# Native sparse attention on one core: queries produced features-first, mask and maximum in one VectorE operation, a pinned TensorE order

## The chip, the cores and the metric

The kernel runs on one core of a Trainium2 chip. The metric is device time in microseconds (us) of one execution. Engines are named as in the profile: PE is TensorE's matmul, PEld its weight load, DVE is VectorE, ACT is ScalarE, POOL is GpSimd, SP is SyncE (here only an issuer of weight loads). All arithmetic is float32 in result; large projections split each float32 operand into a rounded part and a remainder and add three products (`mm3`: high by high, high by low, low by high), so each weight piece has to be turned into `wh` (by ACT) and `wl` (by DVE) before PE can use it.

## The reference, cut to what matters

Two layers, 256 tokens of 1024 features, 16 heads of 64. Layer 0 is stick-breaking attention and an MLP. Then keys and values of three branches are projected once, and layer 1 uses them in native sparse attention:

```
kv = (rms_norm(h, kv_norm) @ w_kv)                # 3 branches x (k, v) x 4 groups x 64
k_cmp, v_cmp = small MLP over 15 blocks of 32 tokens (cmp_pos, cmp_w1, cmp_w2)
k_slc, k_win = partial_rope(kv[.., 1, 0]), partial_rope(kv[.., 2, 0])
proj = rms_norm(h) @ w_q                          # 1024 query features + 48 gates
q, gates = proj[..., :1024], sigmoid(proj[..., 1024:] + gate_b)
q_rot = partial_rope(q)                           # first 16 of 64 features of each head
p_cmp = softmax(q . k_cmp / 8, blocks that have ended)
p_sel = softmax(q_rot . k_slc / 8, causal)        # 4 blocks of 64: all of them are chosen
p_win = softmax(q_rot . k_win / 8, causal)        # window 512 > 256 tokens
out = (gate0 * p_cmp v_cmp + gate1 * p_sel v_slc + gate2 * p_win v_win) @ w_o
```

After it come layer 1's MLP and a final norm.

## The kernel before

**Weights.** All projection weights go through one list, `stream`, in the order of use. `fetch` (L75) issues a load of 1 MB or less on SP's queue, `split` (L87) makes half a piece's `wh` (L96, ACT) and `wl` (L97, DVE), `W(i)` gives a piece to PE and `step` splits ahead by up to three pieces. Only the first load of the program goes out as two half transfers. The loads of layer 0's value weights are cut by `V_CUT` into four pieces of 512 KB and two of 1 MB.

**Banks.** PSUM tiles of 512 columns come from two pools of four: `bank` and `bank2`. A tile that takes a bank over waits until the one before it there has been read.

**Layer 1's attention, `nsa`** (from 301.89 us to the first MLP matmul at 455.51 us). Its parts, in program order, which the scheduler may rearrange on PE:

- `kv_proj(0..2)`: keys and values of the three branches, 48 products of 512 columns each in three passes; the results for the first 128 tokens go out on ACT and for the second on DVE (`evac`). The transposed hidden state is split into `xk` (for kv) and, from the same PSUM tiles `pt`, into `xq` (for q) by `xt_evac`: high part on ACT, low part on DVE, eight of each.
- `gather_tr`/`gather`, `cw_proj`, `cmp_kv`: the block MLP. `cw_proj` is four pieces of weights for little PE work (16 matmuls of 256 columns each).
- `keys_rope` (POOL) and `keys_tr`: rotated keys, transposed into `kT`, split into two rounded parts.
- `q_proj(0..2)`: queries in three pieces of 304, 384 and 384 columns with tokens on the partitions; the 48 gate columns are in the first. Then per pair of heads `q_unrot` (transposes `ptq` into `qTu`, not rotated, for the block scores) and `q_rope` + `q_rot` (rotation on POOL, a split on ACT and DVE into `qsp`, and transposes `ptr` into `qs`).
- `scores(h)`, per head: six matmuls into `z1` (second 128 tokens, 2 x 256 keys) and `z0` (first 128, 2 x 128 keys), of which two add the causal mask; two DVE maxima (L770, L771); four exps on ACT out of PSUM, each with a sum; `scale(h)` divides by the sum and multiplies by the gate on POOL (L790, two operations).
- `turn(h)`: six transposes `ptp` into two tiles, each copied to SBUF. `values(p)`, per pair of heads: eight matmuls into `po` (each appears as two instructions in the profile) and one for the block branch (`pcT`), then `o_evac` (ACT and DVE).
- `cmp_probs`, `cmp_tr`: block softmax of eight heads for the 15 blocks.
- `out_proj`: 96 matmuls of 512 columns. The last `values` runs inside it.

In the steady part the order is scores(h+1), scale(h), turn(h-1), and values of a pair when its second head has been turned.

**Layer 0.** `proj(p)` makes queries and keys of a pair features-first (queries and keys with features on the partitions, 256 columns), `scores`, `turn`, `values` follow one, two and three pairs behind; the last ones are hooks in `out_proj`, at (half, column half, k).

Of the kernel before, what the change touches and what calls it, by code (L numbers as in the profile page):

```python
# [39 lines left out]
def hybrid_kernel(ctx, tc, x, xcols, eye, gcols, gfin, wqk, wv, wo0, wkv, wqa, wqb, wqc, wo1, w1, w2, cw1, cw2, cpos, gate_b, consts, out):  # L40
# [84 lines left out]
    i_kv = [[feed(wkv[n, i], 2048) for i in range(2)] for n in range(3)]  # L125
    i_c = [[feed(cw1[c, i], 2048) for i in range(2)] for c in range(2)]
    i_q = [[feed(w[i], 4 * n) for i in range(2)] for w, n in ((wqa, 304), (wqb, 384), (wqc, 384))]
    i_o1 = [[feed(wo1[n, i], 2048) for n in range(2)] for i in range(2)]
    i_m.append(feed_mlp(1))

    def mm3(o, a, b, first, last):
        nc.tensor.matmul(o, a[0], b[0], start=first, stop=False, skip_group_check=True)  # L132
        nc.tensor.matmul(o, a[0], b[1], start=False, stop=False, skip_group_check=True)  # L133
        nc.tensor.matmul(o, a[1], b[0], start=False, stop=last, skip_group_check=True)  # L134

    def mm(o, a, b, first, last):
        nc.tensor.matmul(o, a, b, start=first, stop=last, skip_group_check=True)  # L137
# [175 lines left out]
    def layer0(ap):  # L313
# [156 lines left out]
    def nsa(xk, pt0, ap):  # L470
# [18 lines left out]
        rstd = []  # L489

        def kv_proj(n, mid=None):
            pk = [bank(f"pk{t}") for t in range(T)]
            for i in range(2):
                w = W(i_kv[n][i])
                if i and mid is not None:
                    mid()
                for kk in range(4):
                    if n == 0 and i == 0 and kk == 2:
                        pts.append(xt_tr(1))
                        xt_evac(pts[1], 1, 4, xk)  # L500
                    if kk % 2 == 0:
                        step()
                    k = 4 * i + kk
                    for t in range(T):
                        mm3(pk[t], tok(xk, k, t), cut(w, kk * 512, (kk + 1) * 512), k == 0, k == NK - 1)
                if n == 0 and i == 0:
                    rstd.extend([rstd_of(hres[t]) for t in range(T)])
            for t in range(T):
                nk = 512 if n == 0 else 256
                dst = kd0[:, t] if n == 0 else kd[n - 1][t]  # L510
                m = nk // DH
                evac(dst, pk[t][:, 0:nk].rearrange("p (m d) -> p m d", m=m)[:, :, None, :].to_broadcast([P, m, 2, DH]), t)
                if n:
                    evac(vs[t][:, n - 1, :], pk[t][:, 256:512], t)
# [4 lines left out]
        def rope(src, t, n):  # L519

            a = ap.tile([P, n, 16], F32, name="ropea", tag=f"ropea{n}")
            b = ap.tile([P, n, 16], F32, name="ropeb", tag=f"ropeb{n}")
            c = cos[:, t:t + 1, :].to_broadcast([P, n, 16])
            nc.gpsimd.tensor_mul(a, src[:, :, 0:16], c)
            s0 = sin[:, t:t + 1, 0:8].to_broadcast([P, n, 8])
            s1 = sin[:, t:t + 1, 8:16].to_broadcast([P, n, 8])
            nc.gpsimd.tensor_mul(b[:, :, 0:8], src[:, :, 8:16], s0)
            nc.gpsimd.tensor_mul(b[:, :, 8:16], src[:, :, 0:8], s1)
            nc.gpsimd.tensor_add(src[:, :, 0:16], a, b)
# [5 lines left out]
        def gather_tr(c):  # L535
            live["g"] = []
            for gp in range(2):
                pt = bank("ptc")
                for g2 in range(2):
                    g = 2 * gp + g2  # L540
                    for t in range(T):
                        nc.tensor.transpose(pt[:, g2 * 256 + t * P:g2 * 256 + (t + 1) * P],
                                            kd0[:, t, c * NG + g].rearrange("p a d -> p (a d)"), ident)
                live["g"].append(pt)

        def gather(c):
            bt = sp.tile([P, 16, M], F32, name="bt", tag="y")
            b = bt.rearrange("p j (g n) -> p j g n", g=NG)
            for gp, pt in enumerate(live["g"]):
# [11 lines left out]
            nc.vector.tensor_sub(bs[:, :, 1, 0:M], bt, f32(bs[:, :, 0, 0:M]))  # L561
# [3 lines left out]
        def keys_rope(br):  # L565
            for t in range(T):
                rope(kd[br][t].rearrange("p g a d -> p (g a) d"), t, 2 * NG)

        def keys_tr(br):
            for t in range(T):  # L570
                pt = bank("ptk")
                for g in range(NG):
                    nc.tensor.transpose(pt[:, g * P:(g + 1) * P], kd[br][t][:, g].rearrange("p a d -> p (a d)"), ident)
                pv = pt.rearrange("p (g k) -> p g k", g=NG)
                kh = kT[0][:, :, br, t * P:(t + 1) * P]
                nc.scalar.copy(kh, pv)
                nc.vector.tensor_sub(kT[1][:, :, br, t * P:(t + 1) * P], pv, f32(kh))
# [38 lines left out]
        nc.vector.tensor_mul(hu, hx, hx)  # L616
        nc.vector.tensor_scalar(hu, hu, 0.044715, 1.0, op0=OP.mult, op1=OP.add)
        nc.vector.tensor_mul(hu, hu, hx)
# [6 lines left out]

        gates = ap.tile([P, T, 48], F32, name="gates")

        def q_proj(n, mid=None):
            cn = 384 if n else 304
            qn = [ap.tile([P, 384], F32, name=f"q{t}", bufs=2)[:, 0:cn] for t in range(T)]  # L630
            pq = [bank(f"pq{t}") for t in range(T)]
            for i in range(2):
                w = W(i_q[n][i])
                if i and mid is not None:
                    mid()
                for kk in range(4):
                    if kk % 2 == 0:
                        step()
                    k = 4 * i + kk
                    for t in range(T):  # L640
                        mm3(pq[t][:, 0:cn], tok(xq, k, t), cut(w, kk * cn, (kk + 1) * cn), k == 0, k == NK - 1)
            for t in range(T):
                evac(qn[t], pq[t][:, 0:cn], t)
            if n == 0:
                for t in range(T):
                    gt = gates[:, t, :]
                    nc.vector.tensor_add(gt, qn[t][:, 256:304], gbs)
                    nc.vector.tensor_scalar(gt, gt, -80.0, None, op0=OP.max)
                    nc.scalar.activation(gt, gt, AF.Exp, scale=-1.0)
                    nc.vector.tensor_scalar(gt, gt, 1.0, None, op0=OP.add)  # L650
                    nc.vector.reciprocal(gt, gt)
            return qn

        def q_unrot(qn, p0, np_):
            for a in range(0, np_, 2):
                m = min(2, np_ - a)
                pt = bank("ptq").rearrange("p (m q) -> p m q", m=2)
                for j in range(m):
                    for t in range(T):
                        nc.tensor.transpose(pt[:, j, t * P:(t + 1) * P], qn[t][:, (a + j) * P:(a + j + 1) * P], ident)  # L660
                nc.scalar.activation(qT[:, p0 + a:p0 + a + m, :], pt[:, 0:m, :], AF.Copy, scale=0.125)

        def q_rope(qn, nh):
            qsp = []
            for t in range(T):
                qv = qn[t][:, 0:nh * DH].rearrange("p (h d) -> p h d", h=nh)
                rope(qv, t, nh)
                s = ap.tile([P, 6, 2, DH], F32R, name="qsp", bufs=2)[:, 0:nh]
                nc.scalar.activation(s[:, :, 0, :], qv, AF.Copy, scale=0.125)
# [331 lines left out]
```

## Time and profile before

| | |
|---|---|
| time, three runs | 639.6, 641.12, 641.71 us (median 641.12) |
| the profiled execution: own time, span in the profile | 642.27 us, 640.4 us |
| TensorE clock granted, mean | 0.999 of full speed |
| busy: PE, DVE, ACT, POOL | 624.8, 435.6, 350.5, 59.6 us |
| layer 0 attention; its MLP; layer 1 attention; its MLP; end | about 0 to 122; to 301.89; to 455.51; to 627; to 640.4 us |

The time of an execution is some 2 us more than its span (what lies before the first and behind the last instruction). The busy time of a matmul overlaps that of the next one, so what an instruction costs is read from one start to the next.

### The profile page before, as it was taken

Reading aid. Unit: us, or ns where it says so; the run is one execution under the profiler, and the core shown is the slowest. Engines: PE = TensorE matmul, PEld = TensorE weight load, DVE = VectorE, ACT = ScalarE, POOL = GpSimd, SP = SyncE. Lnnn points to the kernel's source line nnn. Section 1 sums busy time; section 2 is a strip of 40 time slices with the busy share of each in tenths; the row PEclk is TensorE's granted clock in tenths of the full one; section 3 lists DMA queues with packets and bytes.
Section 4 is the critical chain, followed back from the end, with each engine's and each line's share of the span. In section 5 each row is a group of like instructions: output and inputs, shape, how many; then the busy total and the mean of one; then the engine's idle time right before and its main releaser. Section 6 shows DMA issues by size and latency. Waiting matters only on the chain.

```text
span 640.4 us, 9068 instructions
## 1 busy us (share of the span) xinstructions
PE 624.8 (98%) x3541; PEld 527.9 (82%) x3541; DVE 435.6 (68%) x632; ACT 350.5 (55%) x606; POOL 59.6 (9%) x100
## 2 busy tenths in 40 slices
PE   9999999999999999999999999999999999999995
PEld 6799986888888888888889987777888888888884
DVE  5587887776566665666899879763776566666554
ACT  5666665464444544444847777752564544454433
POOL 0200000000000000000133344550000000000000
PEclk9999999999999999999999999999999999999999
DMA  8953333446555454553465742001545454555501
GB/s 264 409 211 133 132 132 121 151 174 212 197 182 206 160 208 169 201 190 133 150 253 192 258 156 98 3 2 66 198 168 205 162 204 182 198 198 197 198 0 67
DMA packets 17467, 107.86 MB, mean 168 GB/s; under 512 B 2320, under 2 KB 3088, under 8 KB 5648
## 3 DMA queue, kind: packets, MB, share of 16 engines
q1 hardware_dynamic: 16416, 106.03, 46.6%
q10 hardware_dynamic: 1008, 1.25, 0.5%
q8 instruction: 28, 0.46, 0.3%
q14 instruction: 15, 0.12, 0.1%
HBM read 106.22 MB, written 1.05 MB: 168 GB/s over the span
## 4 chain that ended last, share of the span: by engine, by line
PE 75%; DVE 12%; ACT 4%; DMA 4%; issue 3%; POOL 1%; SPq 0%; POOLq 0%; ACTq 0%; DVEq 0%
PE pu L137 27%; PE acc L132 11%; PE acc L133 11%; PE acc L134 11%; DVE wl L97 5%; PE po L137 2%; DMA raw<-in_wv 2%; DVE sbs L430 2%; PE pk L134 2%; PE pk L132 2%; PE pk L133 2%; ACT wh L96 1%; DVE sbe L424 1%; ACT sbs L429 1%; ACT sbs L428 1%
## 5 line engine op out<-in xcount | busy, mean ns | idle before, releaser
L97 DVE TENSOR_TENSOR wl<-raw,wh 128x1024 fp32r<-128x1024 f32 (+3 forms) x204 | 235.1, 1187 | 125.3 <-ACT wh L96 125.1
L96 ACT CAST wh<-raw 128x1024 fp32r<-128x1024 f32 (+3 forms) x204 | 198.5, 1016 | 118.2 <-PE acc L134 50.9
L137 PE MATMUL pu<-xn,wh 128*128 128x512 f32 x512 | 130.1, 392 | 0.6 <-DVE xn L204 0.6
L137 PEld LDWEIGHTS pu<-xn,wh 128*128 128x128 f32 x512 | 93.8, 188 | 19.6 <-DVE xn L204 1.8
L132 PE MATMUL acc<-wh,hh 128*128 128x512 f32 x256 | 100.2, 391 | 0.0
L133 PE MATMUL acc<-wl,hh 128*128 128x512 f32 x256 | 100.1, 391 | 0.0
L134 PE MATMUL acc<-wh,hl 128*128 128x512 f32 x256 | 99.5, 389 | 0.0
L137 PEld LDWEIGHTS pu<-xn,wl 128*128 128x128 f32 x512 | 71.0, 190 | 5.0
L137 PE MATMUL pu<-xn,wl 128*128 128x256 f32 x512 | 74.0, 282 | 0.0
L134 PEld LDWEIGHTS acc<-wh,hl 128*128 128x128 f32 x256 | 48.1, 188 | 10.6 <-DVE hl L293 0.4
L132 PEld LDWEIGHTS acc<-wh,hh 128*128 128x128 f32 x256 | 48.2, 188 | 9.6 <-ACT hh L292 0.6
L133 PEld LDWEIGHTS acc<-wl,hh 128*128 128x128 f32 x256 | 48.2, 188 | 8.8
L292 ACT CAST hh<-ms 128x512 fp32r<-128x512 f32 x32 | 19.9, 620 | 64.7 <-DVE ms L288 64.7
L286 ACT COPY mr<-pu 128x256 f32<-128x256 f32 x64 | 23.6, 369 | 29.2 <-PE pu L137 29.2
L132 PE MATMUL qk<-xa,wh 128*128 128x256 f32 x128 | 37.0, 289 | 0.0
L133 PE MATMUL qk<-xa,wh 128*128 128x256 f32 x128 | 36.2, 283 | 0.0
L134 PE MATMUL qk<-xa,wl 128*128 128x256 f32 x128 | 36.2, 283 | 0.0
L293 DVE TENSOR_TENSOR hl<-ms,hh 128x512 fp32r<-128x512 f32 x32 | 22.1, 692 | 19.9 <-ACT hh L292 19.9
L287 DVE TENSOR_TENSOR mu<-pu,mr 128x256 f32<-128x256 f32 x64 | 26.7, 418 | 5.8 <-ACT mr L286 5.8
L790 POOL TENSOR_TENSOR pe<-pe,rs 128x256 f32<-128x256 f32 (+1 forms) x32 | 27.1, 866 | 23.6 <-DVE rs L786 19.9
L132 PE MATMUL acc<-wh,oT 128*128 128x512 f32 x64 | 25.8, 403 | 0.0
L132 PEld LDWEIGHTS qk<-xa,wh 128*128 128x128 f32 x128 | 24.5, 191 | 1.0 <-issue 0.9
(187 smaller groups left out, 919.7 us busy)
## 6 DMA issues: line engine op xcount, KB each, us to landing
raw<-in_w SPq DMA_DIRECT2D x64, 1024.0 KB, 4.8
raw<-in_wqk SPq DMA_DIRECT2D x8, 1024.0 KB, 6.5
raw<-in_wo SPq DMA_DIRECT2D x8, 1024.0 KB, 4.8
raw<-in_wkv SPq DMA_DIRECT2D x6, 1024.0 KB, 4.8
raw<-in_cw SPq DMA_DIRECT2D x4, 1024.0 KB, 4.8
raw<-in_wv SPq DMA_DIRECT2D x2, 1024.0 KB, 8.1
raw<-in_wv SPq DMA_DIRECT2D x3, 512.0 KB, 5.6
raw<-in_wqb SPq DMA_DIRECT2D x2, 768.0 KB, 4.1
```

The costliest lines, as they stand in the source:

```text
L96: nc.scalar.copy(h[:, r], raws[j][:, r])
L97: nc.vector.tensor_sub(lo[:, r], raws[j][:, r], f32(h[:, r]))
L132: nc.tensor.matmul(o, a[0], b[0], start=first, stop=False, skip_group_check=True)
L133: nc.tensor.matmul(o, a[0], b[1], start=False, stop=False, skip_group_check=True)
L134: nc.tensor.matmul(o, a[1], b[0], start=False, stop=last, skip_group_check=True)
L137: nc.tensor.matmul(o, a, b, start=first, stop=last, skip_group_check=True)
L286: nc.scalar.copy(r[:, q], pu[f][:, 256:512])
L287: nc.vector.tensor_add(u[:, q], pu[f][:, 0:256], r[:, q])
L292: nc.scalar.copy(hh, sv)
L293: nc.vector.tensor_sub(hl, sv, f32(hh))
L430: nc.vector.tensor_tensor_scan(s[:, ::-1], s[:, ::-1], go_on[:, ::-1], 0.0, OP.add, OP.mult)
L790: nc.gpsimd.tensor_tensor(s, s, rs[:, t, :][:, :, None].to_broadcast([P, 2, n]), op=OP.mult)
```

## The change

1. **Queries.** The weights are cut into four pieces of 2048 columns, one for each group of four heads, and `q_proj(g, half)` produces queries with features on the partitions. Both sets of transposes, the splits of rotated queries and the rotation of queries on POOL fall away. The rotation is now: a DVE shuffle of partitions within 32, a DVE product with a sine table, a POOL product with a cosine table, and a DVE sum. The tables are multiplied by the norm's factor of each token, which two matmuls (`pr`) spread over the partitions.
2. **Gates.** Their weights are loaded apart (on ACT's queue) and split early; `gate_proj` has 32 small matmuls after `kv_proj(1)`.
3. **Order of the weight stream.** Pieces of kv, the block MLP and q alternate, so that the short `cw_proj` pieces are apart. Both `gather_tr` stand in `kv_proj(1)`. The split of the blocks' remainder and the keys' rotation (both token halves in one operation) are on POOL. All evacuations of kv are on ACT.
4. **Scores.** Per pair of heads: four float32 matmuls on half the array's rows each, without mask matmuls and without a split of keys or queries. One custom DVE operation (L792) adds the mask, writes negated masked scores to SBUF and reduces to their minimum, with a second instruction that writes out that result: eight such couples for each pair of heads. The exp reads SBUF.
5. **Turns and values.** `turn(p)` has 12 transposes and three copies of 512 columns; values stand four pairs behind scores, and the last four values and two turns stand in `out_proj`. The block branch's value matmul is cut in two of 64 columns.
6. **Order.** From behind `kv_proj(0)` to the end of the scores loop PE's instructions are kept in program order.
7. **Layer 0.** `turn(NP-2)` moves behind 24 matmuls of `out_proj`, and the first seven weight loads go out as halves.

```diff
-            if len(raws) == 1:
+            if len(raws) <= len(V_CUT) + 1:
                 nc.sync.dma_start(raws[-1][:, 0:n // 2], src[:, 0:n // 2])
                 nc.sync.dma_start(raws[-1][:, n // 2:], src[:, n // 2:])
...
+    def pe(ins):
+        if strict[0]:
+            tc.keep_in_program_order(ins)
...
-        out_proj(oT, i_o0, {(0, 0, 2): [lambda: scores(NP - 1), lambda: turn(NP - 2), lambda: values(NP - 3)],
-                            (0, 1, 1): [lambda: values(NP - 2)],
+        out_proj(oT, i_o0, {(0, 0, 2): [lambda: scores(NP - 1), lambda: values(NP - 3)],
+                            (0, 1, 0): [lambda: turn(NP - 2)], (0, 1, 2): [lambda: values(NP - 2)],
...
-                evac(dst, pk[t][:, 0:nk].rearrange("p (m d) -> p m d", m=m)[:, :, None, :].to_broadcast([P, m, 2, DH]), t)
+                nc.scalar.activation(dst, pk[n][t][:, 0:nk].rearrange("p (m d) -> p m d", m=m)[:, :, None, :]
+                                     .to_broadcast([P, m, 2, DH]), AF.Copy, scale=rstd[t])
...
-            nc.vector.tensor_sub(bs[:, :, 1, 0:M], bt, f32(bs[:, :, 0, 0:M]))
+            nc.gpsimd.tensor_sub(bs[:, :, 1, 0:M], bt, f32(bs[:, :, 0, 0:M]))
...
+        pr = bank2("pr")
+        for t in range(T):
+            mm(pr[:, t * P:(t + 1) * P], rstd[t].to_broadcast([P, P]), ident, t == 0, True)
+        for a in range(2):
+            nc.vector.scalar_tensor_tensor(cs[:, a, :], pr[:, 0:T * P], -1.0, cs[:, a, :], op0=OP.mult, op1=OP.mult)
+        kv_proj(1, 0)
+        gather_tr(0)
+        gather_tr(1)
+        kv_proj(1, 1)
+        gather(0)
+        gather(1)
+        gate_proj()
+        keys_rope(0)
+        ph = bank2("ph")
+        kv_proj(2, 0)
+        cw_proj(0, 0)
+        kv_proj(2, 1)
...
+            if half:
+                pq = live.pop(("q", g)).rearrange("p (j q) -> p j q", j=2)
+                nc.scalar.activation(qu[:, g], pq, AF.Copy, scale=0.125)
+                qx = ap.tile([P, 2, T * P], F32, name="qx", bufs=2)
+                nc.vector.stream_shuffle(qx, qu[:, g], swap)
+                nc.gpsimd.tensor_tensor(qr[:, g], qu[:, g], cs[:, 0:1, :].to_broadcast([P, 2, T * P]), op=OP.mult)
+                nc.vector.tensor_tensor(qx, qx, cs[:, 1:2, :].to_broadcast([P, 2, T * P]), op=OP.mult)
+                nc.vector.tensor_add(qr[:, g], qr[:, g], qx)
...
+        def scores(p):
+            g, j = divmod(p, 2)
+            z1 = [bank2(f"z1{hd}").rearrange("p (b k) -> p b k", b=2) for hd in range(2)]
+            z0 = [bank2(f"z0{hd}")[:, 0:256].rearrange("p (b k) -> p b k", b=2) for hd in range(2)]
+            for t, z in ((1, z1), (0, z0)):
+                for hd in range(2):
+                    r = slice(hd * DH, (hd + 1) * DH)
+                    mm(z[hd], qr[r, g, j, t * P:(t + 1) * P], kT[r, g, :, 0:(t + 1) * P], True, True)
...
+                        nc.vector.tensor_tensor_reduce(e, z[hd][:, b, :], nmask[:, 2 * P - n:2 * P], 1.0, 3e38, OP.add, OP.min,
+                                                       nm[:, hd, t, b:b + 1])
+                        nc.scalar.activation(e, e, AF.Exp, scale=-1.0, bias=nm[:, hd, t, b:b + 1],
+                                             accum_out=rs[:, hd, t, b:b + 1])
...
+        scores(0)
+        q_proj(2, 0)
+        scores(1)
+        got = cmp_kv()
+        q_proj(2, 1)
+        scores(2)
+        cmp_kv2(*got)
+        turn(0)
+        q_proj(3, 0)
+        cmp_probs(0)
+        scores(3)
+        turn(1)
+        q_proj(3, 1)
+        cmp_tr(0)
...
+        for p in range(4, NP):
+            scores(p)
+            values(p - 4)
+            turn(p - 2)
...
+        strict[0] = False
```

What moves on the engines is seen at three places. The first is ACT at the end of `kv_proj(0)`, before: `kd` is the block branch's keys and values out of PSUM (one of two, the other being on DVE), `xq` the high part of the queries' input.

```order
L96 CAST wh<-raw 128x1024
L203 ACTIVATE xq<-pt_2617,gc 128x256
L203 ACTIVATE xq<-pt_2618,gc 128x256
L203 ACTIVATE xq<-pt_2688,gc 128x256
L482 ACTIVATE kd_2658<-pk_2662,r 128x1024
L203 ACTIVATE xq<-pt_2689,gc 128x256
L96 CAST wh<-raw 128x1024 x5
```

The same place of the changed kernel:

```order
L96 CAST wh<-raw 128x1024
L532 ACTIVATE kd_2671<-pk_2676,r 128x1024
L532 ACTIVATE kd_2671<-pk_2677,r 128x1024
L219 ACTIVATE xq<-pt_2623,gc 128x256
L219 ACTIVATE xq<-pt_2624,gc 128x256
L219 ACTIVATE xq<-pt_2702,gc 128x256
L219 ACTIVATE xq<-pt_2703,gc 128x256
L96 CAST wh<-raw 128x1024 x5
```

Both `kd` operations, which need the end of `kv_proj(0)` on PE, now stand ahead of the last four `xq`. On PE of the changed kernel the two `pr` matmuls stand right behind `kv_proj(0)`, and everything of the rest of `nsa` behind them:

```order
L145 MATMUL pk_2677<-wh,xk 128x512
L146 MATMUL pk_2677<-wl,xk 128x512
L147 MATMUL pk_2677<-wh,xk 128x512
L150 MATMUL pr<-ident,r 128x128 x2
L145 MATMUL pk_2806<-wh,xk 128x512
L146 MATMUL pk_2806<-wl,xk 128x512
L147 MATMUL pk_2806<-wh,xk 128x512
```

In the kernel before no such matmul stands there. In the changed kernel `pr` takes the bank of the tile `pt_2623`, whose last reader is the low part of the fifth `xq` on DVE, which follows that `xq` on ACT (a wait on the operation that stands there in the built program).

The second place is POOL from the queries of group 1 to those of group 2 (`qr` is a query group's product with the cosine table, `pe` a pair's probabilities, `hv` a copy for the block branch), in the changed kernel:

```order
L678 TENSOR_TENSOR qr<-qu,cs 128x512 x2
L803 TENSOR_TENSOR pe<-pe,rs 128x512 x2
L803 TENSOR_TENSOR pe<-pe,rs 128x256 x2
L709 COPY hv<-hidT 128x480
L803 TENSOR_TENSOR pe<-pe,rs 128x512 x2
L803 TENSOR_TENSOR pe<-pe,rs 128x256 x2
L678 TENSOR_TENSOR qr<-qu,cs 128x512
```

The scales of pairs 0 and 1 and the copy `hv` stand between the second and third `qr`. Before, POOL had there the scale of one head and the rotation of the third query piece for both halves of the tokens (`q_3349` and `q_3350`):

```order
L790 TENSOR_TENSOR pe<-pe,rs 128x256
L790 TENSOR_TENSOR pe<-pe,rs 128x512
L524 TENSOR_TENSOR ropea<-q_3349,cst 128x96
L527 TENSOR_TENSOR ropeb<-q_3349,cst 128x6x8
L528 TENSOR_TENSOR ropeb<-q_3349,cst 128x6x8
L529 TENSOR_TENSOR q_3349<-ropea,ropeb 128x6x16
```

There, one head's scale stood ahead of the rotation; now it is four heads' scales and a copy.

The third place is DVE of the changed kernel at pair 2's scores (`z_3453` and `z_3454`: the second 128 tokens of its two heads, two branches each; `qx` the shuffled queries of group 2):

```order
L677 STREAM_SHUFFLE qx<-qu 128x512
L792 ISA pe,nm<-z_3453,nmask 128x256
L792 ISA nm 128x1
L679 TENSOR_TENSOR qx<-qx,cs 128x512
L792 ISA pe,nm<-z_3453,nmask 128x256
L792 ISA nm 128x1
L680 TENSOR_TENSOR qr<-qr,qx 128x512
L792 ISA pe,nm<-z_3454,nmask 128x256
L792 ISA nm 128x1
L792 ISA pe,nm<-z_3454,nmask 128x256
L792 ISA nm 128x1
```

Before, DVE had at its scores one maximum for all of a head's `z1` and one for its `z0`:

```order
L770 TENSOR_REDUCE nm<-z_3564 128x2
L771 TENSOR_REDUCE nm<-z_3565 128x2
L784 RECIPROCAL rs<-rs 128x4
L728 TENSOR_REDUCE cmx<-psc 128x8
L786 TENSOR_TENSOR rs<-rs,gates 128x4
```

The sum `qr`, which waits for POOL's third product, now stands ahead of six of pair 2's eight mask-and-maximum operations. PE's `pvc` (the block branch's values), `turn(0)` and all behind them wait for the fourth of these, since `pvc` takes over the bank of `z_3454`.

## Rows read from the trace of the kernel before

**Rows 1.** Busy time by stretch: us, then PE, PEld, DVE, ACT, POOL, PEclk, DMA share, GB/s

```profile
302.00:345.00 43.00, 42.13 (x228) 36.09 (x227) 39.80 (x50) 30.83 (x47) 13.58 (x22) 1.00 0.52 180
345.00:382.00 37.00, 35.44 (x246) 33.20 (x245) 30.99 (x56) 24.68 (x52) 12.29 (x22) 1.00 0.65 228
382.00:400.00 18.00, 16.54 (x135) 13.21 (x136) 16.68 (x52) 13.20 (x49) 9.21 (x13) 1.00 0.23 87
400.00:432.00 32.00, 31.29 (x233) 23.07 (x230) 22.73 (x66) 21.73 (x93) 17.88 (x23) 1.00 0.01 2
```

**Rows 2.** PE's waits from 300 to 456 us: total, times, longest

```profile
PE z L137 <- ACT pe L775: 1.4, 2, 0.7
PE ptk L573 <- POOL kd L529: 0.9, 1, 0.9
```

**Rows 3.** Timeline of PE: start us, duration us, then the instruction; 384-column products, `ptr`

```profile
363.63 0.33 PE L133 MATMUL pq<-wl,xq 128*128 128x384 f32 x1
363.81 0.34 PE L134 MATMUL pq<-wh,xq 128*128 128x384 f32 x1
363.98 0.80 PE L680 MATMUL ptr<-ident_r,qsp 128*128 128x128 f32 x8
364.62 0.62 PE L137 MATMUL pkc<-hidT,w2d 128*128 128x60 f32 x4
```

**Rows 4.** Timeline of PE, steady part of the scores: values, a turn, a head's scores

```profile
415.26 1.60 PE L137 MATMUL po<-pT,vs 128*64 128x256 f32 x16
416.79 0.70 PE L137 MATMUL po<-pcT,vcb 60*128 60x256 f32 x2
417.42 0.33 PE L799 MATMUL ptp<-ident,pe 128*128 128x128 f32 x1
...
418.05 0.71 PE L137 MATMUL z<-kT,qs 128*128 128x512 f32 x2
...
419.09 0.27 PE L799 MATMUL ptp<-ident,pe 128*128 128x128 f32 x1
```

**Rows 5.** Timeline of PE in layer 0: 256-column products, a pair's scores

```profile
71.75 0.28 PE L133 MATMUL qk<-xa,wh 128*128 128x256 f32 x1
71.87 0.28 PE L134 MATMUL qk<-xa,wl 128*128 128x256 f32 x1
72.08 0.92 PE L137 MATMUL z<-qkT 64*128 64x256 f32 x8
72.94 0.44 PE L442 MATMUL pa<-ident,sbe 128*128 128x128 f32 x2
```

**Rows 6.** PE's waits from 0 to 122 us

```profile
PE pv L132 <- ACT wh L96: 1.5, 1, 1.5
...
PE pa L442 <- ACT sbe L432: 1.1, 2, 0.8
```

**Rows 7.** Timeline of ACT: layer 0's split of a 1 MB value piece

```profile
18.37 2.00 ACT L96 CAST wh<-raw 128x1024 fp32r<-128x1024 f32 x2 [2.70 <-DMA raw<-in_wv]
```

**Rows 8.** Timeline of ACT at the end of `kv_proj(0)`

```profile
313.26 1.12 ACT L482 ACTIVATE kd<-pk,r 128x1024 f32<-128x1024 f32 x1
314.28 0.46 ACT L203 ACTIVATE xq<-pt,gc 128x256 fp32r<-128x256 f32 x1
314.63 1.99 ACT L96 CAST wh<-raw 128x1024 fp32r<-128x1024 f32 x2
```

**Rows 9.** Timeline of POOL: the keys' rotation, beside DVE's `wl`

```profile
327.41 1.26 POOL L524 TENSOR_TENSOR ropea<-kd,cst 128x128 f32<-128x128 f32 x1
...
331.27 0.46 POOL L529 TENSOR_TENSOR kd<-ropea,ropeb 128x128 f32<-128x128 f32 x1
```

**Rows 10.** POOL's groups, 300 to 432 us: busy, mean ns, then idle before and releaser

```profile
L790 POOL TENSOR_TENSOR pe<-pe,rs 128x512 f32<-128x512 f32 x16 | 17.1, 1066 | 0.0
L790 POOL TENSOR_TENSOR pe<-pe,rs 128x256 f32<-128x256 f32 x16 | 10.6, 665 | 23.6 <-DVE rs L786 19.9 <-ACT q L482 3.7
```

**Rows 11.** Timeline of DVE: a head's maxima

```profile
404.71 0.68 DVE L770 TENSOR_REDUCE nm<-z 128x2 f32<-128x512 f32 x1
405.31 0.41 DVE L771 TENSOR_REDUCE nm<-z 128x2 f32<-128x256 f32 x1
405.64 0.17 DVE L784 RECIPROCAL rs<-rs 128x4 f32<-128x4 f32 x1
```

**Rows 12.** Groups of DVE (380 to 432 us) and of ACT (302 to 432 us), one each

```profile
L728 DVE TENSOR_REDUCE cmx<-psc 128x8 f32<-128x120 f32 x4 | 1.1, 276 | 0.9 <-PE psc L137 0.8
...
L775 ACT ACTIVATION_READ_ACCUMULATOR pe<-z,nm 128x1 f32 x32 | 6.4, 201 | 0.0
```

**Rows 13.** DVE's group of weight splits, 302 to 382 us

```profile
L97 DVE TENSOR_TENSOR wl<-raw,wh 128x1024 fp32r<-128x1024 f32 x23 | 28.7, 1274 | 2.9 <-ACT wh L96 2.8
```

More of the change, by code (lines that the diff above doesn't have):

```diff
@@ L489, in nsa, with kv_proj @@
         rstd = []
[L491 to L507, printed above, removed]
+        pk = {}
+        def kv_proj(n, i):
+            if i == 0:
+                pk[n] = [bank(f"pk{t}") for t in range(T)]
+            w = W(i_kv[n][i])
+            for kk in range(4):
+                if n == 0 and i == 0 and kk == 2:
+                    pts.append(xt_tr(1))
+                    xt_evac(pts[1], 1, 4, xk)
+                if kk % 2 == 0:
+                    step()
+                k = 4 * i + kk
+                for t in range(T):
+                    mm3(pk[n][t], tok(xk, k, t), cut(w, kk * 512, (kk + 1) * 512), k == 0, k == NK - 1)
+            if n == 0 and i == 0:
+                rstd.extend([rstd_of(hres[t]) for t in range(T)])
+            if i == 0:
+                return
             for t in range(T):
@@ L623, in nsa @@
         nc.vector.tensor_mul(hu, hu, hx)
[L626 to L669, printed above, removed]
-                nc.vector.scalar_tensor_tensor(s[:, :, 1, :], qv, 0.125, f32(s[:, :, 0, :]),
-                                               op0=OP.mult, op1=OP.subtract)
-                qsp.append(s)
-            return qsp
@@ L702, in cmp_kv2 @@
         def cmp_kv2(hidT, hv):
-            pc = bank("pkc")
+            pc = bank2("pkc")
             for e in range(2):
@@ new lines, in cmp_probs @@
+            n = 8 * T
+            pv = pc[:, 0:T * 120].rearrange("p (h n) -> p h n", h=n)
+            mx = ap.tile([P, n], F32, name="cmx")
+            nc.vector.tensor_reduce(mx, pv, axis=AX.X, op=OP.max)
+            e = ap.tile([P, n, NC], F32, name="ce", bufs=2)
+            nc.vector.tensor_tensor(e, pv, mx[:, :, None].to_broadcast([P, n, NC]), op=OP.subtract)
+            for t in range(T):
+                nc.scalar.activation(e[:, 8 * t:8 * t + 8, :], e[:, 8 * t:8 * t + 8, :], AF.Exp, scale=rstd[t])
@@ new lines, in turn @@
+        def turn(p, bk=bank):
+            pes = live.pop(("e", p))
+            pT = ap.tile([P, 12 * P], F32, name="pT", bufs=2)
+            for i in range(3):
+                pt = bk("ptp")
+                for m in range(4):
+                    hb, c = divmod(4 * i + m, 3)
+                    hd, b = divmod(hb, 2)
+                    o = (512 + b * P, b * 256, b * 256 + P)[c]
+                    tr(pt[:, m * P:(m + 1) * P], pes[hd][:, o:o + P])
+                if i == 1:
+                    nc.vector.tensor_copy(pT[:, 512 * i:512 * (i + 1)], pt)
+                else:
+                    nc.scalar.copy(pT[:, 512 * i:512 * (i + 1)], pt)
+            live["t", p] = pT
@@ L809, in values @@
+        def values(p, bk=bank):
             g = p // 2
-            po = bank("po1")
-            pT = [live.pop(("t", 2 * p + hd)) for hd in range(2)]
+            po = bk("po1")
+            pT = live.pop(("t", p))
             for b in range(2):
```

331 lines of the change are left out of this document (149 added, 182 removed).

## The prediction

> **What bounds the kernel now.** I read the busy time by stretch first. PE is the bound nearly everywhere: in layer 1's attention its idle time is 0.87, 1.56, 1.46 and 0.71 us in four stretches up to 432 us, 4.6 us in all, at the full clock (PEclk 1.00, the 2.4 GHz level) [rows 1]. So the change earns what it takes out of PE, and loses what new waits put in. Second, PE's waits: the longest are scores for the exps that free their banks and keys for POOL's rotation [rows 2]. DVE is next in line: 16.68 of 18 us from 382 to 400, but 22.73 of 32 us in the steady part [rows 1]. ACT and POOL have room. Outside this layer two places count: layer 0's start, where PE waits 1.5 us for a split behind a 1 MB load, and one turn that waits 0.8 us [rows 6, 7].
>
> **What goes from PE.** Costs are from start to start.
> - 32 `ptr` transposes: eight take 0.64 us, so 2.6 us [rows 3]. 16 `ptq`: by the turn's six in 0.63 us, 0.105 each, 1.7 us [rows 4].
> - Scores: a head costs 1.04 us now (418.05 to 419.09), a pair 2.08 [rows 4]. The new form is layer 0's: half the rows, no mask; 768 columns take 0.86 us there, so 1536 take 1.72 [rows 5]. The values' 16 instructions, also 1536 columns at half the array, take 1.53 [rows 4]. I take 1.65, nearer the same form: 0.43 a pair, 3.4 us (2.9 to 4.4).
> - The block branch's value matmul: 0.63 us now; as two halves by the values' rate (512 of 1536 columns) 0.51: 1.0 us for eight pairs (0 to 1.0) [rows 4].
> - Query products: 384 columns take 0.17 us, 304 in proportion 0.14, so 96 and 48 of them 23.3 us; 192 of 256 columns at just under 0.12, say 0.118, take 22.7: 0.6 us [rows 3, 5].
> - Added: 32 gate matmuls of 96 or 48 columns. The nearest rows are `ptr` with 0.08 (128 columns) and 0.12 for 256: I take 0.08, 2.6 us (1.3 by columns alone, 3.8) [rows 3, 5]. `pr`, four instructions by a transpose's 0.105: 0.4 us.
>
> Together 6.3 us less work. If nothing new waits, the 4.6 us of idle time go too. Adding the spacings up from 347.55 to 404.35 us leaves some 2.3 us that are neither work nor listed wait, where transposes, scores and block softmax alternate; half of it, 1.2, I count as going (0 to 2.3).
>
> **Layer 0.** With half loads ACT can split the first half of the 1 MB piece before the second lands; of the 1.5 us I take 1.3 (0 if the loads together are limited by the transfer rate) [rows 6, 7]. The moved turn hides its 0.8 us behind 24 products; with it 0.7. Together 2.0 us.
>
> No new wait: 6.3 + 4.6 + 1.2 + 2.0 = 14.1 us less.
>
> **What the new order adds.** PE's order is pinned now, so a wait at its head stops all of it.
> 1. *`pr`.* It follows `kv_proj(0)` and takes a bank whose last reader is the fifth low part of `xq`, which follows ACT's fifth high part. That one now stands behind both `kd` operations, 1.02 us each from start to start, and these need the end of `kv_proj(0)`; the first started at 313.26 [rows 8]. So: 313.3 + 2 x 1.02 + 0.35 for the high part + 0.4 for DVE's part = 316.1, with the releases 316.3, while PE is free at 313.7: 2.6 us (1.6 if `kd` overlaps more, 3.4 if a weight split gets between). Before, one `kd` was on DVE and nothing on PE waited.
> 2. *The first `cw_proj`.* The blocks' remainder stands on POOL behind the keys' rotation (four operations, now twice as long). A rotation step takes 0.46 us alone and 1.26 beside DVE's `wl` [rows 9]. From the end of the key evacuations, some 2 us behind `kv_proj(1)` (four operations of half or a quarter of `kd`'s columns), rotation takes about 5 us and 960 columns of remainder 2.0 (512 take 1.07, rows 10); PE gets there after gates and half of `kv_proj(2)`, 2.6 + 5.5 us. 1.0 us late (0 to 2.5).
> 3. *Pairs 0 to 2.* From the end of the second query chunk as 0: scores of pair 0 to 1.65, half a query chunk (24 x 0.118) to 4.5. Meanwhile DVE has two halves of a weight split (1.27 each [rows 13]), the GELU steps, group 1's rotation and eight mask-and-maximum couples, one after another: I take 0.42 us for 256 columns with its read and 0.30 for 128 (below). The eighth ends at 6.8, another `wl` at 7.9, and the second operation on pair 1's first tile ends at 8.9; `pht` takes over that tile's bank. PE would have been there at 6.1: 2.8 us. Half a chunk and pair 2's scores end at 13.7; `pkc` waits until 15.0 for pair 2's first tile: 1.3 us. Then DVE reaches the sum `qr` of group 2, whose product stands on POOL behind pair 0's scales (from 8.9: 2 x 1.07 + 2 x 0.67 = 3.5), `hv` (0.6), pair 1's (3.5), and its own 1.07 [rows 10]: 17.6. DVE waits for it, from about 14.9, with pair 2's third and fourth operation queued behind; these end at 18.8, and `pvc`, `turn(0)` and the next query chunk stand until then, from 15.5: 3.3 us. Together 7.4 us (5 to 10).
>
> Later pairs: PE per pair 1.65 + 1.53 + 0.51 + 1.26 (12 transposes) = 4.95 us, DVE eight couples for 2.9, a copy of 0.6 and some 0.65 of small ones, 4.15; POOL 3.5; ACT's exps now read SBUF, and it has room. So PE bounds again, and pair 3's and group 3's waits lie behind query products.
>
> **The unknown price** is the mask-and-maximum couple. Lower bound: a maximum of 256 columns starts 0.33 us before the next operation (405.31 to 405.64) and lasts 0.41; 120 columns last 0.28 [rows 11, 12]; with no cost for the read 4 x 0.33 + 4 x 0.22 = 2.2 us a pair. Upper bound: full durations and a read such as ACT's, 0.20 [rows 12]: 4 x 0.41 + 4 x 0.28 + 8 x 0.20 = 4.4. I take 2.9, nearer to DVE's own rows, as DVE shows no read here.
>
> The Trainium skill ("VectorE: DVE Perf Modes", rules for kernel authors and the section on the DRAIN) speaks against this step: fusing is not done for speed, since the pipe empties after each operation, and the number of operations should be kept low. Here the number goes from four maxima a pair to eight couples. Row 405.31 has the next operation 0.08 us before the first one's end, so the trace agrees only in part; by the rule alone the pair would cost the upper bound.
>
> **The sum.** 642.27 (own time of the profiled execution, 1.15 above the median) - 14.1 + 2.6 + 1.0 + 7.4 = 639.2; against the median 638.0. About 0.3% (1.9 us) is what a measurement of this kernel can tell from no change, so this is a small gain, 0.5%.
>
> **The rivals.**
> - *No new wait bites.* If POOL and DVE queue less than I walked, and `pr`'s and `qr`'s waits are short, 14.1 us are won: 627.0 us. For it: DVE has 9.3 us to spare from 400 to 432, POOL 14 [rows 1]. Against: the three waits stand in the built order, and their durations are this trace's. 0.16.
> - *DVE becomes the bound in the scores: slower.* With 4.4 us for the couples DVE needs 5.65 a pair against PE's 4.95: 0.7 for each of the last six pairs, 4.0 us; and the 20 couples ahead of `pvc` cost 1.5/8 more each, 3.7 us. 645.7. It decides from about 3.7 us a pair on; above 3.9 the time is behind the old one. For it: the couple's second instruction, and the pages' rule above. Against: the short rows of DVE. 0.18.
> - *The gain is eaten.* Layer 0 gives nothing since its start is bound by the transfer rate (+2.0), and the gates cost 0.12 each (+1.2): 641.2, no change. 0.16.
>
> **How the numbers follow.** My own case has 0.50, from 634 to 641: 0.40 of it faster by over 0.3% (below 639.2), 0.10 within. With the first rival 0.56 faster; the third (0.14) and my rest 0.24 the same; the second and a little of the third 0.20 slower. The range reaches from the first rival's 626, if all idle time goes, to the second's 645.5: 626 to 645.5.
>
> **What would show it.** Right: PE idle about 2.6 us ahead of `pr` with DVE `xq` as releaser; about 3 us each ahead of `pht` and `pvc`, with DVE's `nm` as releaser, and POOL's product `qr` late; a DVE idle of 2 to 3 us ahead of `qr`; pairs of 5.0 us from pair 4 on, without idle. `pv`'s wait in layer 0 below 0.3 us. Wrong: couples over 0.45 us on average, with PE waiting for `nm` in every pair (the second rival); a scores pair that still takes 2 us; gate matmuls over 0.12; or waits on ACT's exps, to which I gave nothing.

## The result, and the profile after

The changed kernel takes 648.99 us (median of four runs, 647.88 to 650.14) where the kernel before takes 640.54 (639.60 to 641.71): a ratio of 1.0131, 95% interval 1.0105 to 1.0157. It is 8.45 us slower; a gain of 3.1 us was forecast.

The profiled execution (649.01 us, span 647.2, 6.8 above that of before) puts the loss in one place. Layer 1's attention runs from 300.64 to 462.43 us, 161.8 us where it was 153.6; it starts 1.25 us earlier (layer 0), and what follows it takes the same time. First PE's waits in that layer, in the view of [rows 2]:

```profile
PE pvc L150 <- DVE nm L792: 3.8, 1, 3.8
PE pr L150 <- DVE xq L220: 2.9, 1, 2.9
PE pkc L150 <- DVE nm L792: 1.9, 1, 1.9
PE pht L705 <- DVE rs L798: 1.4, 1, 1.4
PE z L150 <- DVE nm L792: 0.7, 2, 0.4
PE z L150 <- ACT pcT L763: 0.2, 1, 0.2
```

10.9 us in all. The four longest stand at places that were walked to, behind the releasers that were named; for `pht` the view names `rs`, which stands on DVE right behind the `nm` that was meant. The fifth place, the first `cw_proj`, has no wait. The second thing was in no term. PE's busy time and granted clock by stretch, with the columns of [rows 1] for PE alone (us, busy, PEclk, DMA share, GB/s):

```profile
300.00:312.00 12.00, 12.00 (x59) 1.00 0.42 141
312.00:316.00 4.00, 1.13 (x5) 0.92 0.74 262
316.00:320.00 4.00, 4.00 (x15) 0.66 0.12 20
320.00:366.00 46.00, 46.00 (x312) 1.00 0.59 221
366.00:382.00 16.00, 12.40 (x80) 1.00 0.39 150
382.00:386.00 4.00, 0.23 (x2) 0.70 0.00 0
386.00:390.00 4.00, 4.00 (x27) 0.50 0.01 4
390.00:394.00 4.00, 4.00 (x35) 0.95 0.00 2
```

Before, PEclk is 1.00 in every stretch of this layer [rows 1]. Now it drops twice towards 0.50 (the 1.2 GHz level): behind the wait ahead of `pr`, and in and behind the waits ahead of `pkc` and `pvc`. PE counts as busy for all of 386 to 390, and does its work at half speed.

The same on PE's timeline (start, duration, the instruction; what it waited in brackets):

```profile
377.92 1.56 PE L150 MATMUL z<-kT,qr 64*128 64x512 f32 x8
381.33 0.63 PE L150 MATMUL pkc<-hidT,w2d 128*128 128x60 f32 x4 [1.85 <-DVE nm L792]
385.77 1.93 PE L150 MATMUL pvc<-cw2s,hv 128*60 128x64 f32 x16 [3.81 <-DVE nm L792]
387.63 2.82 PE L153 MATMUL ptp<-ident,pe 128*128 128x128 f32 x12
```

Twelve transposes take 2.82 us here and 1.53 at full clock later. What DVE and POOL did meanwhile, each on its own timeline, POOL's first:

```profile
374.59 4.16 POOL L803 TENSOR_TENSOR pe<-pe,rs 128x512 f32<-128x512 f32 x4 [5.74 <-DVE rs L798]
378.70 0.59 POOL L709 COPY hv<-hidT 128x480 f32<-128x480 f32 x1
379.25 3.62 POOL L803 TENSOR_TENSOR pe<-pe,rs 128x512 f32<-128x512 f32 x4
382.84 1.26 POOL L678 TENSOR_TENSOR qr<-qu,cs 128x512 f32<-128x512 f32 x1
```

```profile
384.13 0.69 DVE L680 TENSOR_TENSOR qr<-qr,qx 128x512 f32<-128x512 f32 x1 [2.95 <-POOL qr L678]
384.74 0.42 DVE L792 CUSTOM_DVE_ANT_0 pe<-z,nmask 128x256 f32<-128x256 f32 x1
385.08 0.08 DVE L792 DVE_READ_ACCUMULATOR2_ANT nm<- 128x1 f32 x1
385.08 0.42 DVE L792 CUSTOM_DVE_ANT_0 pe<-z,nmask 128x256 f32<-128x256 f32 x1
```

The queries' product of group 2 ran on POOL from 382.84, behind two pairs' scales and `hv`; DVE stood 2.95 us for it, with the two operations for which `pvc` waited queued behind. On ACT the two `kd` stand ahead of the `xq` for which `pr` waited, as in the order shown above:

```profile
312.28 2.15 ACT L532 ACTIVATE kd<-pk,r 128x1024 f32<-128x1024 f32 x2
314.28 1.61 ACT L219 ACTIVATE xq<-pt,gc 128x256 fp32r<-128x256 f32 x4
```

And the work itself, to be read against [rows 4]: the gates and what follows them, the scores of pairs 0 and 1, and a pair in the steady part.

```profile
330.22 3.65 PE L150 MATMUL pg<-wgp,xq 128*128 128x96 f32 x32
333.71 0.49 PE L145 MATMUL pk<-wh,xk 128*128 128x512 f32 x1
...
365.60 1.56 PE L150 MATMUL z<-kT,qr 64*128 64x512 f32 x8
...
370.16 1.12 PE L150 MATMUL z<-kT,qr 64*128 64x512 f32 x2
371.62 1.52 PE L150 MATMUL z<-kT,qr 64*128 64x512 f32 x6 [0.34 <-DVE nm L792]
...
421.79 2.00 PE L150 MATMUL z<-kT,qr 64*128 64x512 f32 x8
423.71 1.52 PE L150 MATMUL po<-pT,vs 128*64 128x256 f32 x16
425.16 0.65 PE L150 MATMUL po<-pcT,vcb 60*64 60x256 f32 x4
425.74 1.53 PE L153 MATMUL ptp<-ident,pe 128*128 128x128 f32 x12
```

### The profile page after: what moved, and what is told of

Its sections match the earlier page's. It is cut to its first block, busy times and chain, and to the rows that moved or that the text cites. A ratio compares the mean times of both kernels' runs of the same rounds, so it can differ in the third digit from the quotient of the medians.

```text
span 647.2 us, 9100 instructions
## 1 busy us (share of the span) xinstructions
PE 625.8 (97%) x3561; PEld 524.7 (81%) x3561; DVE 428.5 (66%) x672; ACT 354.7 (55%) x603; POOL 57.0 (9%) x76
## 4 chain that ended last, share of the span: by engine, by line
PE 81%; ACT 6%; DVE 5%; issue 2%; POOL 2%; DMA 2%; SPq 0%; POOLq 0%; ACTq 0%; DVEq 0%
PE pu L150 27%; PE acc L145 11%; PE acc L146 11%; PE acc L147 11%; PE po L150 3%; DVE wl L97 3%; ACT pe L794 2%; POOL pe L803 2%; ACT wh L96 2%; PE z L150 1%; PE qk L145 1%; PE pk L145 1%; PE pk L146 1%; PE pk L147 1%; PE ptp L153 1%
## 5 line engine op out<-in xcount | busy, mean ns | idle before, releaser
L97 DVE TENSOR_TENSOR wl<-raw,wh 128x1024 fp32r<-128x1024 f32 (+1 forms) x200 | 240.3, 1238 | 120.8 <-ACT wh L96 120.6
L96 ACT CAST wh<-raw 128x1024 fp32r<-128x1024 f32 (+1 forms) x200 | 197.9, 1031 | 104.7 <-PE acc L147 46.4
L803 POOL TENSOR_TENSOR pe<-pe,rs 128x512 f32<-128x512 f32 (+1 forms) x32 | 31.2, 1007 | 27.9 <-ACT pT L820 14.8
L794 ACT ACTIVATE pe<-pe,nm 128x256 f32<-128x256 f32 (+1 forms) x64 | 28.3, 444 | 7.0 <-DVE nm L792 6.9
```

Of the source, the lines that this page charges most:

```text
L96: nc.scalar.copy(h[:, r], raws[j][:, r])
L97: nc.vector.tensor_sub(lo[:, r], raws[j][:, r], f32(h[:, r]))
L794: nc.scalar.activation(e, e, AF.Exp, scale=-1.0, bias=nm[:, hd, t, b:b + 1], accum_out=rs[:, hd, t, b:b + 1])
L803: nc.gpsimd.tensor_tensor(sv, sv, rs[:, hd, t, :][:, :, None].to_broadcast([P, 2, n]), op=OP.mult)
```

## The experiments

Theory: the three waits and the half clock behind them are the loss, and both come from results that are late on ACT, DVE and POOL and meet a PE order that can't step aside. Rivals: the waits are handed on when one is removed; the new work on PE is what costs; the clock falls for another reason.

**e1: `pr` later.**

```diff
-        pr = bank2("pr")
...
         kv_proj(1, 0)
+        pr = bank2("pr")
```

> The two pr matmuls stand behind the first half of kv_proj(1) instead of ahead of it. Waits and clock (my theory): PE's 2.9 us wait ahead of pr goes, and with it the half clock behind it (granted 0.50 from 316 to 318 us, 0.81 from 318 to 320: 1.4 us): 4.3 us less, about 644.7 us. Rival, the wait is only handed on (DVE and ACT are as late for pairs 0 to 2 as before): under 1.5 us less, 647.5 or more, with larger waits ahead of pht, pkc or pvc.

Measured: 643.97 us (642.02 to 646.32), ratio to before 1.0049 (1.0031 to 1.0067): 5.0 us less. No wait ahead of `pr` is left, the waits ahead of `pht`, `pkc` and `pvc` stay at 1.3, 1.8 and 3.8 us. The wait wasn't handed on. (In the trace the clock now fell at another place, from 329 to 333 us; e5 takes that up. Of the ten executions four took 645.6 to 646.3 us with a mean granted clock of 0.989, the traced one among them, and six 642.0 to 644.0 us with 0.991 to 0.994, so such a dip need not stand in every execution.)

**e2: the product on DVE.**

```diff
-                nc.gpsimd.tensor_tensor(qr[:, g], qu[:, g], cs[:, 0:1, :]...
+                nc.vector.tensor_tensor(qr[:, g], qu[:, g], cs[:, 0:1, :]...
```

> The queries' product with the cosine table is on DVE instead of POOL. Waits and clock: DVE no longer waits 2.95 us for POOL ahead of the sum qr, PE's wait ahead of pvc falls from 3.8 to 1.5 us or less, and the half clock from 384 to 390 us (3.4 us lost) goes for the most part: 4 to 6 us less, 643 to 645 us. Rival, DVE is the bound there: the four added operations of 0.6 us keep pvc's wait above 3 us and the time at 648 to 650.

Measured: 650.51 us, ratio 1.0146 (1.0120 to 1.0172); the rival's number, and its wait: `pvc` still waits 4.0 us. PE's listed waits are 10.2 us in all, for 10.9 in the changed kernel; what rose is the loss by the clock, with a mean of 0.981 to 0.984 over the four executions for 0.986 to 0.989. DVE no longer waits for POOL, but it is slowed by it. DVE's timeline of this kernel, beside POOL's scales:

```profile
377.09 3.70 DVE L97 TENSOR_TENSOR wl<-raw,wh 128x1024 fp32r<-128x1024 f32 x2
...
382.75 1.16 DVE L678 TENSOR_TENSOR qr<-qu,cs 128x512 f32<-128x512 f32 x1
383.84 1.52 DVE L679 TENSOR_TENSOR qx<-qx,cs 128x512 f32<-128x512 f32 x1
385.28 0.41 DVE L792 CUSTOM_DVE_ANT_0 pe<-z,nmask 128x256 f32<-128x256 f32 x1
```

Two splits take 3.70 us, and products of 512 columns 1.16 and 1.52, where such a product takes 0.68 and a split 1.21 with POOL idle (changed kernel, 362.46 and 364.38 us). So neither engine's queue had room at that place.

**e3: `pr` later, and the rotation of groups 2 and 3 issued later.** e1's edit is in it; the rotation's four operations now stand in a function, `q_rope`.

```diff
+                if g < 2:
+                    q_rope(g)
...
         turn(0)
+        q_rope(2)
         q_proj(3, 0)
...
             turn(p - 2)
+            if p == 4:
+                q_rope(3)
```

> pr late, and the rotation of the query groups 2 and 3 issued after turn(0) and after turn(2), with its product still on POOL. Waits and clock: both long waits and both stretches of half clock go, 2.9 + 1.4 + 3.8 + 3.4 = 11.5 us less at most, 638 to 640 us, about the kernel before. Rival, the new work on PE is what costs (gates 3.5 us, scores of 1.9 to 2.2 us a pair): the time stays above 644 us.

Measured: 637.68 us (636.49 to 639.88), ratio 0.9954 (0.9937 to 0.9972): 11.3 us less than the changed kernel, and faster than before. PE's largest waits in the layer:

```profile
PE pht L709 <- DVE rs L802: 1.4, 1, 1.4
PE z L150 <- DVE ce L750: 0.8, 1, 0.8
PE pkc L150 <- DVE nm L796: 0.7, 1, 0.7
```

The new work is not what made the kernel slower than before: all of it is still there.

**e4: the idle stretches filled.** Matmuls whose results nobody reads stand in the waits; the waited-for results come no earlier.

```diff
+        fill(12)
         pr = bank2("pr")
...
+            fill(8)
             pc = bank2("pkc")
...
+            fill(16)
             pvc = bank2("pvc")
```

> The changed kernel with idle PE filled: 12 matmuls of 512 columns ahead of pr, 8 ahead of pkc and 16 ahead of pvc, whose results nobody reads. Each fill is about as long as the wait that it stands in, so the waits stay (as work). If the clock falls because of the idle stretches, it now stays at 1.00 and the 4.8 us of half clock come back: about 644 us. Rival, the clock falls for another reason or its loss is hidden: 648 to 650 us, clock still below 1.00 behind the fills.

Measured: 645.59 us (644.29 to 646.20), ratio 1.0064 (1.0039 to 1.0090): 3.4 us less, with more work. The stretches that fell before:

```profile
312.00:316.00 4.00, 3.84 (x19) 1.00 0.57 236
316.00:320.00 4.00, 4.00 (x20) 1.00 0.40 113
...
382.00:386.00 4.00, 3.88 (x37) 1.00 0.00 0
386.00:390.00 4.00, 4.00 (x37) 1.00 0.54 178
```

So the idle time does pull the clock down, and this costs 3.4 us, or rather more: the fills and the waits that are left last about 0.5 us longer together than the waits did. The two timelines agree: from the first `pk` to the first `z` the changed kernel takes 64.96 us and this one 63.41; from there to the first `psc` 27.61 and 25.44: 3.7 us together.

**e5: wide gates on top of e3.** The gates with features on the partitions: 16 matmuls of 256 columns and two transposes for 32 short ones.

```diff
-                    mm(pg[:, t * 96:(t + 1) * 96], h, wgp[:, k].rearrange("p a c -> p (a c)"), k == 0 and t == 0, False)
-                    mm(pg[:, t * 96:t * 96 + 48], lo, wgp[:, k, 0, :], False, k == NK - 1)
+                mm(pg[0:96, 0:256], wgp[:, k].rearrange("p a c -> p (a c)"), xq[0][:, k, :], k == 0, False)
+                mm(pg[0:48, 0:256], wgp[:, k, 0, :], xq[1][:, k, :], False, k == NK - 1)
```

> On top of e3 (637.7 us): the gates are produced features-first, 16 matmuls of 256 columns and two transposes instead of 32 matmuls of 96 or 48 columns. If the short matmuls themselves let the clock fall behind them (0.50 to 0.69 for four microseconds, PE listed as busy all the time), it now stays at 1.00: 1.4 us of work and 1.7 us of clock less, about 634.6 us. Rival, the clock there follows from the earlier short idle or the transposes: only the 1.4 us of work go, 636.3 us, and the dip stays.

Measured: 636.86 us (635.05 to 638.74), ratio 0.9930 (0.9907 to 0.9954); against e3 the intervals overlap, so a gain of 0.8 us is not established. The stretch of the gates, e3's row first and e5's in the fence behind:

```profile
324.00:328.00 4.00, 4.00 (x36) 1.00 0.00 0
328.00:332.00 4.00, 4.00 (x13) 0.57 0.73 262
```

```profile
324.00:328.00 4.00, 4.00 (x27) 1.00 0.05 20
328.00:332.00 4.00, 4.00 (x20) 1.00 0.69 225
```

In e3 PE has no wait there and the clock still fell, right behind 32 matmuls of 96 or 48 columns; in e5 it did not. But e5 lost it at 368 to 372 us (0.57), behind the wait of 1.35 us ahead of `pht`, which in e3 was as long and had left it at 1.00. The expectation was half right: the dip left the gates and came back elsewhere.

**e6: group 1's rotation behind pair 0's scores, on top of e3.**

```diff
-                if g < 2:
+                if g < 1:
                     q_rope(g)
...
         scores(0)
+        q_rope(1)
         q_proj(2, 0)
```

> On top of e3 (637.7 us): the rotation of query group 1 is issued behind the scores of pair 0, so the eight mask-and-maximum operations of pair 0 stand together on DVE. If pair 1's scores and pht wait for DVE's place in its queue, their waits (0.3 + 1.4 us, and 1.2 us inside pair 1's matmuls) fall by about 1.5 us: 636.2 us. Rival, DVE's amount of work in that stretch decides, not its order: the same 1.5 us appear ahead of pair 2's scores or pkc, no change.

Measured: 638.89 us (636.77 to 642.38), ratio 0.9961 (0.9942 to 0.9981), no gain over e3. The wait ahead of `pht` rose from 1.4 to 2.9 us, and the 0.3 + 1.2 us that pair 1's scores had lost are gone: `pht` starts 9.0 us behind the first scores, 8.9 in e3. So the amount of DVE's work decides there, not its order, and the wait only moved. My theory of that wait fell. (Behind it the clock fell, to 0.58 from 372 to 376 us.)

**e7: the kernel before with layer 0's two edits alone.**

```diff
-            if len(raws) == 1:
+            if len(raws) <= len(V_CUT) + 1:
...
-        out_proj(oT, i_o0, {(0, 0, 2): [lambda: scores(NP - 1), lambda: turn(NP - 2), lambda: values(NP - 3)],
-                            (0, 1, 1): [lambda: values(NP - 2)],
+        out_proj(oT, i_o0, {(0, 0, 2): [lambda: scores(NP - 1), lambda: values(NP - 3)],
+                            (0, 1, 0): [lambda: turn(NP - 2)], (0, 1, 2): [lambda: values(NP - 2)],
```

> The kernel before with the two edits of layer 0 alone: seven loads in halves, the turn moved. Forecast had 2.0 us for them; in the trace of the changed kernel layer 1 starts 1.25 us earlier. So 1 to 2 us faster than before. Rival, the start is bound by the transfer rate and the turn's wait reappears later: no change.

Measured: 640.47 us against 641.25, ratio 0.9987 (0.9973 to 1.0000). About 0.8 us, at the edge of what can be told; 2.0 were forecast.

**e8: e3 without the pinned order.**

```diff
-        strict[0] = True
```

> e3 (637.7 us) without the pinned PE order. My theory: the waits come from what stands ahead on DVE, ACT and POOL, and the scheduler's own order of PE does not know their times either: 637 to 642 us, other waits of the same size. Rival, the pinned order is what makes a wait expensive: 2 us or more below e3.

Measured: 637.46 us (635.75 to 637.65), ratio 0.9934 (0.9915 to 0.9953); against e3 no difference that can be told.

**e10: the changed kernel without the pinned order**, the same one line taken out.

> The changed kernel (649.0 us) with one edit: the pinned order taken away. The scheduler then places pr 16 matmuls (3.6 us) later and turn(0) ahead of pvc; DVE's and POOL's queues are as before. If the pinned order turned the two late results into idle PE, pr's wait goes and pvc's falls from 3.8 to about 2 us, with part of the half clock: 641 to 644 us. Rival, the queues alone decide: 647 to 650 us with the same waits under other names.

Measured: 642.57 us (640.37 to 643.99), ratio 1.0020 (1.0007 to 1.0033): 6.4 of the 8.45 us lost are gone by this line. The scheduler put `pr` 16 matmuls later and `turn(0)` between `pkc` and `pvc`:

```profile
377.25 0.63 PE L150 MATMUL pkc<-hidT,w2d 128*128 128x60 f32 x4 [1.14 <-DVE nm L791]
377.71 1.49 PE L153 MATMUL ptp<-ident,pe 128*128 128x128 f32 x12
382.41 1.07 PE L150 MATMUL pvc<-cw2s,hv 128*60 128x64 f32 x16 [2.98 <-DVE nm L791]
```

`pr` has no wait left; `pvc` still has one, as DVE and POOL are as late as before, and the clock falls behind it (0.59 from 384 to 388 us) and behind the gates (0.66 from 328 to 332). So with late results the pinned order costs; with the results in time (e3, e8) no cost of it can be told.

**e9: e5 without the pinned order**, the same line again; all repairs together.

> e5 (636.9 us) without the pinned PE order: the version with every repair. The pinned order is not what costs, so about e5 again or up to 1.5 us less, 635.3 to 637 us, clearly faster than the kernel before. Rival: with the free order the wide gates' transposes or pht are put where they wait, 638 us or more.

Measured: 635.91 us (635.17 to 636.83), ratio 0.9922 (0.9909 to 0.9936): 4.8 us faster than before, 13 us faster than the changed kernel. In the trace the clock is 1.00 in all of the layer.

**e11: e5 with six matmuls in the wait ahead of `pht`.**

```diff
+            fill(6)
             pt = bank2("pht")
```

> e5 (636.9 us) with six matmuls of 512 columns (1.4 us) in PE's wait ahead of pht, behind which e5's clock fell to 0.57 from 368 to 372 us. If that wait is what lets the clock fall, it stays at 1.00 and 1.5 us come back: 635.4 us. Rival, the dip comes again elsewhere behind short transposes, as it did from e3 to e5: no change, 636.5 to 637.5 us.

Measured: 636.49 us (636.10 to 637.41), ratio 0.9931 (0.9918 to 0.9945). The dip is gone, the time is e5's within the intervals. What that dip cost can't be told from no cost.

## Why the prediction was wrong

The waits were right nearly one by one: `pr` 2.6 forecast and 2.9 measured; `pht` with pair 1's scores 2.8 and 1.7 (and 1.2 more inside the matmuls, below); `pkc` 1.3 and 1.9; `pvc` 3.3 and 3.8; the first `cw_proj` 1.0 and none. Together 11.0 and 10.9, with 0.5 in pairs 4 and 5, which no term had. e1 and e3 show that removing the two longest removes the loss, and e10 that most of the loss needs the pinned order. That `pr` is late by the two `kd` ahead of `xq` on ACT is read from the order and the timeline; no run turns them round.

POOL's queue with the scales ahead of `qr` ended at 384.1, 18.5 us behind the first scores; 17.6 had been walked. The walk to `pht` ended right, 8.9 us behind the first scores in both, but partly by luck: its eight couples took 2.2 us for 2.9 and one half split fell into it for two, while the GELU steps and the rotation took some 2 us more than was left for them. "PE bounds again" held for the later pairs, but from pair 4 on they took 5.4 to 6.3 us, block softmax left out, for 4.95 forecast, and one sign of being wrong came true: scores pairs that still take 2 us.

The unknown price was sized too high, and this was not the loss: a mask-and-maximum couple takes 0.34 us for 256 columns and 0.21 for 128 from start to start, its read included, 2.2 us a pair, the lower bound. With that price the rival "DVE becomes the bound in the scores" did not happen, though its time of 645.7 us was nearest. The rule behind it in the Trainium skill ("VectorE: DVE Perf Modes", the DRAIN you can't avoid) is that the next operation does not start until the pipe is empty; the same section says that one which is not held, that is, not made to wait for all before it, starts earlier. For the couples the trace agrees with the second: the read starts 0.08 us before its operation's listed end (385.08 for 384.74 + 0.42), and the next operation starts with the read.

One term was missing, one group of terms was sized too large by far, and a third term probably so.

1. *The sum priced an idle stretch at its own length.* The prediction read "at the full clock (PEclk 1.00 ...)" from before and kept it for the new order. The two long idle stretches let the clock fall to 1.2 GHz for work that stood behind them: 3.4 us by e4's time, 3.7 by its timeline. The Trainium skill ("TensorE: Matmul & The Clock Gate", what's actually happening) says that the gate follows how busy PE has been lately, and that an idle PE goes back to half rate; e4's runs agree, but it had no place in the sum. This is a missing term, as large as the gain forecast.
2. *"What goes from PE", 6.3 us and 1.2 of small gaps.* Of these 7.5 us, 1.9 are found: 161.8 us less 10.9 of waits and 3.7 of clock are 147.2, against 153.6 less 4.5 of waits, 149.1.

   The largest miss is the scores. Where the banks of both heads are free, the two heads' matmuls, on half the rows each, run beside each other, and a pair takes 1.5 to 1.7 us (pairs 0, 2 and 3), as the 1.65 forecast. Where the second head's bank comes late, they run one behind the other, and little of that is listed as a wait: in pair 1 (lines above) the first head's two instructions take 1.12 us alone and the other six 1.52, where pair 0's eight take 1.56 together. Pair 1 took 3.0 us with 0.3 listed, pairs 4 to 7 took 2.4, 2.9, 2.2 and 1.9 with 0.5 listed; the view names DVE's `nm` for pair 5 and ACT's `pcT` for pair 4. All eight took 16.2 us without the listed waits, for 13.2 forecast. Before, the scores took 18.1 counted the same way, so 1.9 us were won for 3.4.

   The gates took 3.49 us (330.22 to 333.71) for 2.6 forecast, inside the bounds. The rest comes from adding up PE's steps by tile, from start to start without the waits, before and in e4 (the changed kernel's work at clock 1.00): query products 0.2 us more instead of 0.6 less; `out_proj`'s own matmuls 0.8 more, with more values and turns among them; turns and block softmax 1.0 more; against this, transposes and `cw_proj` 0.9 better than forecast. With the 1.2 us of gaps, for which no tile shows a gain, these make some 5.3 of the 5.6 us that are missing. No run was made for them one by one.
3. *Layer 0, 2.0 us.* 1.25 in the trace, and about 0.8 by e7's times, whose interval ends at 1.7. The sign "`pv`'s wait in layer 0 below 0.3 us" failed in the changed kernel's trace, with 0.9 us for `wh` and 0.8 for `wl` where it was 1.5; e7's trace has 0.3. The traces scatter: in the twelve with this layer 0, layer 1 starts 1.0 to 2.8 us earlier than in the one of before, so a pair of traces does not size this term.

With 3.7 + 5.6 + 0.75, the span's 6.8 us more follow from the 3.1 less that were forecast (10.0 against 9.9). The second and third alone would have made it 3.2 us slower; the clock and they together made it clearly slower. The first rival, "no new wait bites", is what e3, e5 and e9 come near, with 4 to 5 us of short waits left: 635.9 to 637.7 us instead of 627.0, as most of the 5.6 us of work was still not saved.

## What to carry to other kernels

An order of instructions that is pinned on the bound engine turns late results of other engines into idle time that a free order can partly fill (6.4 us here): pin it only when the results are in time, and read from the other engines' queues what stands ahead of each result that the pinned engine meets. Price a long idle stretch of PE at its length and the half-clock work behind it (here 3.4 us for 8.6 us of idle time), and look at the granted clock behind such a place before anything else. When a product can be computed any time before it is needed, issue it where it is needed, not where it becomes possible: e3, with e1's edit in it, moved no work to another engine and won 11.3 us. And where two matmuls share the array's rows, look whether both banks come free together (pair 0 against pair 1): if one is late, the price of the pair goes up without a wait to show for it.

## What was not expected of the hardware

- The clock fell behind 3.5 us of 96- and 48-column matmuls (e3: 0.57 from 328 to 332 us), with PE counted as busy all the time and without a wait since 318.6 us. The traces of e1, e2, e6 and e10 have a dip at the same place; those of the changed kernel, e4 and e8, with the same gates, have none, nor have the three with wide gates. That the short matmuls are the cause is therefore not shown. What decides stays open, as does why a wait of 1.35 us let the clock fall in e5 and not in e3.
- POOL slows DVE, as DVE slows POOL [rows 9]: beside POOL's scales a DVE product of 512 columns from SBUF took 1.16 to 1.52 us instead of 0.68, and a split 1.85 instead of 1.21 (e2), while the couples, one operand of which lies in PSUM, kept their 0.41. The Trainium skill ("SBUF — State Buffer", who interferes with whom) says that a DVE instruction with two SBUF inputs contends with a POOL instruction that reads SBUF; the rows agree on which operations are slowed.
